# Value weights folded into the output weights, in an encoder layer of attention and mLSTM

## The chip, the cores and the metric

The kernel runs on one core of one Trainium2 chip (trn2). The metric is device time in microseconds (us), the median of a few executions. PE is the engine for matmuls, DVE (VectorE), ACT (ScalarE) and POOL (GpSimd) work on tiles of 128 partitions, and SP (SyncE) issues most DMAs. SPq and ACTq are the queues of DMAs that SP and ACT issue.

## What is computed

```python
def mla_group(c_q, c_kv, k_pe, cos, sin, g_cq, g_ckv, w_uq, w_ukv, g_q, g_k):
    q = (rms_norm(c_q, g_cq) @ w_uq).reshape(B, S, A_HEADS, A_DH)
    kv = (rms_norm(c_kv, g_ckv) @ w_ukv).reshape(B, S, A_HEADS, A_NOPE + A_DV)
    k_nope, v = kv[..., :A_NOPE], kv[..., A_NOPE:]
    ...
    # softmax(q k^T * scale) v per head, all queries see all keys

def reference(x, ...):
    h = rms_norm(x, g_mix_norm[l])
    z = h @ w_in[l]
    q_m, k_m, v_m, o_m, gates, c_q, c_kv, k_pe = jnp.split(z, splits, axis=-1)
    ...
    y_a = mlstm_group(q_m, k_m, v_m, o_m, gates, b_gates[l], g_mlstm_out[l])
    y_b = mla_group(c_q, c_kv, k_pe, cos, sin, ...)
    x = x + jnp.concatenate([y_a, y_b], axis=-1) @ w_out[l]
    h = rms_norm(x, g_ffn_norm[l])
    x = x + jnp.square(jax.nn.relu(h @ w_ff1[l])) @ w_ff2[l]
```

There are 2048 tokens, a model width of 1024, four attention heads with 128 value columns, 128 key columns and 64 rotary columns each, and a latent `c_kv` of 128 columns, from which keys and values of all heads are made. All in float32.

## The kernel before

Every float32 product is made of three matmuls: each operand is split into a high part (`kh`, a cast on ACT) and the rest (`kl`, a subtraction on DVE or POOL), by `split`, and `mm3` adds high x high, low x high and high x low. "A product" below is three such matmuls, if nothing else is said.

The first phase makes the input projection z for the two halves of the tokens. A half has three blocks (`CV`, `CQ`, `CO`: value, query-and-key, out-gate columns) of eight token tiles each. A slot is one such tile, 24 matmuls. Into the slots `tick` sets the stages of the attention's latent work for a token tile t: `mla_a1` normalises the latents (`cn`), transposes and splits them (`cTh`, `cTl`); `mla_a2` multiplies them by the split weights `wukh`, `wukl` (128 x 1024: for each head 128 key and 128 value columns) in two products of 512 columns, `pk`; `mla_b1` copies the value columns out of `pk` (`vn`, on ACT) and stores them to `d_va` in DRAM; `mla_b2` transposes queries and keys and stores them (`d_qn`, `d_qr`, `d_kn`, `d_kr`). In this phase a scheduler sets the order of instructions on each engine. The out-gate slots end in a sigmoid and a store `d_sg<-vo`.

Attention follows, in the order in which it is written. It runs 16 blocks (four heads by four query blocks of 512 queries), 16 scores each; g counts the 256 scores. A score is five matmuls of 128x512 (three for the 128 key columns, two for the rotary ones, `rh`, `rl`, `qr`) into one of three banks `ps`. DVE copies it out and takes its maximum (`p`), ACT takes exponentials, PE transposes the probabilities, ACT and DVE split them (`pth`, `ptl`), and PE multiplies them with a split value block (`vh`, `vl`) in `pv`, 22 scores later. `load_q`, `load_k` and `load_v` bring raw queries, keys and values of a head into tiles `raw` of a pool of eight stage tiles; `split_q`, `split_k` and `split_v` split them. At the start `load_q(0, 0)`, the four `load_k(0, j)` and their splits stand ahead of everything else; later heads are loaded and split at fixed scores. The mLSTM group runs between the scores, as a generator `work`; its first part is `mlstm_prelude`. After attention, `OutProj` multiplies by `w_out` (rows 0 to 511 for mLSTM, the rest for attention), and the feed-forward layers follow.

A tile may lie on memory of another one that is no longer read; then the first instruction that writes it waits for the last one that read the old tile. Each DMA also takes one of eight completion lanes in turn (`DMAHW0` to `DMAHW7` in the order's rows) and waits until the DMA that had the lane before has landed.

## Time and profile before

| | |
|---|---|
| median of 3 runs | 2543.5 us (2543.17 to 2545.29) |
| profiled execution | 2542.08 us |
| its span in the trace | 2540.3 us |
| granted clock of PE | 1.00 |
| PE busy | 2523.7 us (99%) |
| DVE busy | 1726.1 us (68%) |
| ACT busy | 1293.7 us (51%) |
| POOL busy | 380.7 us (15%) |

Times inside the kernel are counted from the start of the span. The first phase ends and attention begins at about 458 us; attention ends at about 1122 us. Busy shares are averages over these stages.

### The profile page before, as it was taken

The page shows a single profiled execution, that of the slowest core. Times are in us where ns is not written, and L with a number is a line of the kernel's source. Part 1 is how long each engine was busy: PE and PEld are TensorE (multiplying, and loading weights), DVE is VectorE, ACT ScalarE, POOL GpSimd, SP SyncE. Part 2 cuts the span into 40 slices and gives each one's busy share as a digit, 9 for nine tenths or more (in the row PEclk, how much of TensorE's full clock was granted, in tenths as well). Part 3 has the DMA queues.
Part 4 walks back from the last instruction along what each step waited for, and adds up shares of the span by engine and source line. Part 5 has one row for each costly group of instructions (what it writes and reads, how often), then busy time and mean ns, then how long its engine had stood idle before and what let it go on. Part 6 is the DMA issues. An engine that isn't in the chain of part 4 may idle for free. (4 is left out here: it accounts for less than half of the span.)

```text
span 2540.3 us, 35812 instructions
## 1 busy us (share of the span) xinstructions
PE 2523.7 (99%) x12380; PEld 2111.3 (83%) x12380; DVE 1726.1 (68%) x3286; ACT 1293.7 (51%) x2900; POOL 380.7 (15%) x428
## 2 busy tenths in 40 slices
PE   9999999999999999999999999999999999999999
PEld 7888888788888888888888888888888888888887
DVE  5585467766667667678788777977775577665433
ACT  6454444656767677674455555655554323332332
POOL 1211111223323332200000000000000232322000
PEclk9999999999999999999999999999999999999999
DMA  5434234355344343235786555654448544444552
GB/s 177 143 112 152 91 113 137 111 146 134 89 115 114 85 121 102 63 110 193 235 271 227 196 189 185 244 166 149 142 153 300 201 149 142 145 145 145 211 183 95
DMA packets 295931, 392.53 MB, mean 155 GB/s; under 512 B 32262, under 2 KB 176965, under 8 KB 295749
## 3 DMA queue, kind: packets, MB, share of 16 engines
q1 hardware_dynamic: 293284, 385.78, 48.0%
q10 hardware_dynamic: 2464, 4.46, 0.5%
q8 instruction: 97, 1.59, 0.3%
q14 instruction: 86, 0.70, 0.1%
HBM read 258.51 MB, written 131.64 MB: 154 GB/s over the span
## 5 line engine op out<-in xcount | busy, mean ns | idle before, releaser
L69 PE MATMUL pd<-w2h,uh 128*128 128x512 f32 x896 | 348.8, 389 | 0.1
L70 PE MATMUL pd<-w2l,uh 128*128 128x512 f32 x896 | 348.7, 389 | 0.0
L71 PE MATMUL pd<-w2h,ul 128*128 128x512 f32 x896 | 348.7, 389 | 0.0
L54 DVE TENSOR_TENSOR ul<-ur,uh 128x1024 fp32r<-128x1024 f32 x110 | 149.3, 1357 | 251.8 <-ACT uh L53 251.8
L53 ACT CAST uh<-ur 128x1024 fp32r<-128x1024 f32 x110 | 115.7, 1052 | 396.0 <-PE pd L70 382.4
L54 DVE TENSOR_TENSOR ptl<-ptp,pth 128x512 fp32r<-128x512 f32 x248 | 171.1, 691 | 190.0 <-ACT pth L53 188.9
L53 ACT CAST pth<-ptp 128x512 fp32r<-128x512 f32 x248 | 143.4, 578 | 157.7 <-PE ptp L1137 157.1
L2015 DVE TENSOR_TENSOR e<-pu,e 128x512 f32<-128x512 f32 x224 | 151.3, 689 | 88.7 <-PE pu L71 87.7
L69 PEld LDWEIGHTS pd<-w2h,uh 128*128 128x128 f32 x896 | 168.2, 188 | 35.4 <-DVE e L2015 0.5
L71 PEld LDWEIGHTS pd<-w2h,ul 128*128 128x128 f32 x896 | 168.2, 188 | 34.9
L70 PEld LDWEIGHTS pd<-w2l,uh 128*128 128x128 f32 x896 | 168.2, 188 | 34.8
L1106 ACT ACTIVATE p<-p,nm 128x512 f32<-128x512 f32 x256 | 185.8, 726 | 2.6 <-DVE nm L1099 2.6
L1095 DVE TENSOR_SCALAR_CACHE_REDUCE p<-ps 128x512 f32<-128x512 f32 x256 | 167.4, 682 | 15.2 <-PE ps L1094 15.1
L2179 POOL TENSOR_TENSOR r<-wr,r 128x512 f32<-128x512 f32 x48 | 81.5, 1697 | 621.1 <-DMA wr<-in_w 590.0
L69 PE MATMUL pz<-wh,hh 128*128 128x512 f32 (+1 forms) x384 | 149.5, 391 | 1.7 <-ACT vo L495 0.7
L71 PE MATMUL pz<-wh,hl 128*128 128x512 f32 (+1 forms) x384 | 150.0, 391 | 0.0
L70 PE MATMUL pz<-wl,hh 128*128 128x512 f32 (+1 forms) x384 | 149.2, 389 | 0.1
L2018 ACT ACTIVATE e<-e 128x512 f32<-128x512 f32 x128 | 80.9, 632 | 120.5 <-DVE e L2015 114.0
L1137 PE MATMUL ptp<-ident,p 128*128 128x128 f32 x992 | 130.6, 274 | 0.5 <-DVE ptl L54 0.3
L1137 PEld LDWEIGHTS ptp<-ident,p 128*128 128x128 f32 x992 | 113.6, 140 | 14.1 <-issue 1.4
L1090 PE MATMUL ps<-kh,qh 128*128 128x512 f32 x256 | 112.8, 441 | 2.4 <-DVE p L1095 2.4
L1883 ACT CAST r<-w1raw 128x512 fp32r<-128x512 f32 x104 | 64.6, 622 | 92.5 <-PE pu L71 92.5
(526 smaller groups left out, 6463.5 us busy)
## 6 DMA issues: line engine op xcount, KB each, us to landing
d_u<-e SPq DMA_DIRECT2D x224, 256.0 KB
ur<-d_u SPq DMA_DIRECT2D x110, 512.0 KB
wr<-in_w SPq DMA_DIRECT2D x96, 256.0 KB
w1raw<-in_w SPq DMA_DIRECT2D x42, 512.0 KB
raw<-in_w_in SPq DMA_DIRECT2D x48, 256.0 KB
r<-in_w SPq DMA_DIRECT2D x22, 512.0 KB
mb<-d_M SPq DMA_DIRECT2D x32, 256.0 KB
acc<-d_x SPq DMA_DIRECT2D x16, 512.0 KB
```

The lines of the kernel that those rows point to most:

```text
L53: r = nc.scalar.copy(hi, src)
L54: (eng or nc.vector).tensor_tensor(lo, src, hi.bitcast(F32), op=ALU.subtract)
L69: nc.tensor.matmul(out, ah, bh, start=first, stop=False, skip_group_check=more)
L70: nc.tensor.matmul(out, ah, bl, start=False, stop=False, skip_group_check=more)
L71: nc.tensor.matmul(out, al, bh, start=False, stop=last, skip_group_check=more)
L1090: nc.tensor.matmul(o, qh[:, qs], kh, start=True, stop=False)
L1095: nc.vector.tensor_scalar(p, o, SCALE, None, op0=ALU.mult, op1=ALU.max, accum_out=maxes[b, a][:, j:j + 1])
L1106: nc.scalar.activation(p, p, AF.Exp, bias=maxes[b, a], accum_out=dens[b][:, a, j:j + 1])
L1137: nc.tensor.transpose(pt[:, k, :], p[:, k * P:(k + 1) * P], c.ident)
L2015: nc.vector.tensor_tensor(out, o, t, op=ALU.add)
L2018: nc.scalar.activation(t, t, AF.Relu)
L2179: nc.gpsimd.tensor_tensor(R, wr, R, op=ALU.subtract)
```

## The change

Attention's result of a head is the weighted sum of value rows, and these are latents times the head's value weights. The head's rows of `w_out` come behind. The changed kernel multiplies the two weights once, W'(h) = W_value(h) x W_out(h) (128 x 1024), and lets attention sum latents.

- `load_wu` splits only the key columns of `w_ukv` into the first 512 columns of `wukh` and `wukl`; `mla_a2` makes one product of 512 columns for keys. `mla_b1` no longer copies and stores values. `mla_a2` stores the 128 latent columns of `cn` to `d_cn`, on ACT's queue.
- `value_rows` runs in the slots n = 13 to 23 of the second half, one step a slot: it loads `w_ukv` again, scales and transposes its value columns (four transposes), splits them into the other 512 columns of `wukh` and `wukl`, loads `w_out`'s rows of the heads in eight pieces, splits each into a token tile `xt`, and makes eight products of 128x512, one a slot. Each result is copied on ACT and stored to `d_wv` on ACT's queue.
- Attention loads four value blocks once for all heads, from `d_cn`, in place of four for each head. Their loads stand at g = 2 to 8 and their splits (cast on ACT, subtraction on POOL) at g = 16 to 22; before, they were loaded ahead of the scores and split at g = 6 to 12, and again for each head at the end of the one before.
- The split of the next head's key block 2 (u = 5) goes from POOL to DVE.
- The mLSTM's first loads of values and keys come at the eleventh step of the prelude, no longer ahead of it, and later ones at the step before.
- `OutProj` reads `d_wv` where it read rows 512 and on of `w_out`.

```diff
             for j in range(2):
-                raw = rp.tile([P, 512], F32, name="raw")
-                cs = slice(j * 512, (j + 1) * 512)
-                nc.sync.dma_start(raw, c.w_ukv[:, cs])
-                split(nc, wukh[:, cs], wukl[:, cs], raw, gcq[:, 2:3])
+                raw = load_ukv(j)
+                cs = slice(j * 256, (j + 1) * 256)
+                split(nc, *[w[:, cs].rearrange("p (h d) -> p h d", h=2) for w in (wukh, wukl)],
+                      raw[:, :, 0, :], gcq[:, 2:3])
+
...
+        def value_rows():
+            raws = [load_ukv(j) for j in range(2)]
+            yield
+            for raw in raws:
+                nc.scalar.activation(raw[:, :, 1, :], raw[:, :, 1, :], AF.Copy, scale=gcq[:, 2:3])
+            pt = psT.tile([P, 4, P], F32, name="pt")
+            for h in range(NH):
+                nc.tensor.transpose(pt[:, h, :], raws[h // 2][:, h % 2, 1, :], c.ident)
+            split(nc, wukh[:, 512:], wukl[:, 512:], pt.rearrange("p h d -> p (h d)"))
+            yield
+            pieces = {}
+
+            def load(n):
+                h, j = divmod(n, 2)
+                pieces[n] = rp.tile([P, 512], F32, name="raw")
+                nc.sync.dma_start(pieces[n], c.w_out[512 + h * P:512 + (h + 1) * P, j * 512:(j + 1) * 512])
+
+            def part(n):
+                t = xp.tile([P, D], F32R, name="xt")
+                wh, wl = t[:, 0:512], t[:, 512:D]
+                split(nc, wh, wl, pieces.pop(n))
+                if 0 < n and n + 3 < 2 * NH:
+                    load(n + 3)
+                parts.append((wh, wl))
+
+            parts = []
+            load(0)
+            part(0)
+            yield
+            for n in range(1, 4):
+                load(n)
+            for n in range(2 * NH):
+                h, j = divmod(n, 2)
+                if n + 1 < 2 * NH:
+                    part(n + 1)
+                wh, wl = parts.pop(0)
+                o = psM.tile([P, 512], F32, name="pm")
+                hs = slice(512 + h * P, 512 + (h + 1) * P)
+                mm3(nc, o, wukh[:, hs], wukl[:, hs], wh, wl, True, True)
+                w = ep.tile([P, 520], F32, name=("ot", "zc")[j])[:, 0:512]
+                nc.scalar.copy(w, o)
+                nc.scalar.dma_start(c.d_wv[h * P:(h + 1) * P, j * 512:(j + 1) * 512], w)
+                yield
...
-            zr, ms3, ch, cl = mla_env[t]
-            pk, pq = [], []
-            for j in range(2):
-                o = psM.tile([P, 512], F32, name="pm")
-                cs = slice(j * 512, (j + 1) * 512)
-                mm3(nc, o, ch[:, 2, :], cl[:, 2, :], wukh[:, cs], wukl[:, cs], True, True)
-                pk.append(o)
+            zr, ms3, ch, cl, cn = mla_env[t]
+            nc.scalar.dma_start(c.d_cn[t * P:(t + 1) * P, :], cn[:, 256:384])
+            pq = []
+            pk = psM.tile([P, 512], F32, name="pm")
+            mm3(nc, pk, ch[:, 2, :], cl[:, 2, :], wukh[:, 0:512], wukl[:, 0:512], True, True)
...
-            vn = mp.tile([P, NH, DV], F32, name="vn")
-            for j in range(2):
-                nc.scalar.copy(vn[:, 2 * j:2 * j + 2, :],
-                               pk[j].rearrange("p (h d) -> p h d", h=2)[:, :, NOPE:])
-            nc.sync.dma_start(c.d_va[tok, :], vn.rearrange("p h d -> p (h d)"))
...
                     tick(n + 6 * half)
+                    if half and n >= 13:
+                        next(rows, None)
...
-        load_v(0, 0)
-        load_v(0, 1)
         work = mlstm()
...
                 if h < NH - 1 and i == 7 and u in (4, 5, 6):
-                    split_k(h + 1, u - 3, nc.vector if u == 6 else nc.gpsimd)
-                    if u == 6:
-                        load_v(h + 1, 0)
-                        load_v(h + 1, 1)
+                    split_k(h + 1, u - 3, nc.gpsimd if u == 4 else nc.vector)
...
-                if g in (6, 8, 10, 12):
-                    split_v(0, g // 2 - 3)
-                    if g < 10:
-                        load_v(0, g // 2 - 1)
+                if g in (2, 4, 6, 8):
+                    load_v(g // 2 - 1)
+                if g in (16, 18, 20, 22):
+                    split_v(g // 2 - 8)
...
-            nc.sync.dma_start(raw, c.w_out[k * P:(k + 1) * P, :])
+            nc.sync.dma_start(raw, c.d_wv[(k - 4) * P:(k - 3) * P, :])
```

The order in which SP issues DMAs shows where the loads of attention's first tiles stand (`raw<-d_qn` and `raw<-d_qr` are its queries, `raw<-d_kn` and `raw<-d_kr` its keys; the names in brackets are what an instruction waits for, a lane first). In the kernel before they begin among the last stores of the latent attention's queries (L407):

```order
L1064 DMA raw_4984<-d_qn_78 128x512 [waits DMAHW2_49,PE_49]
L1067 DMA raw_4986<-d_qr_80 64x512 [waits DMAHW3_49]
L1067 DMA raw_4986<-d_qr_80 64x512 [waits DMAHW4_49]
L1033 DMA raw_4989<-d_kn_79 128x512 [waits DMAHW5_49]
L1036 DMA raw_4991<-d_kr_81 64x512 [waits DMAHW6_49]
L407 DMA d_qn_78<-qT_4378 128x4x128 [waits DMAHW7_49,Activation_49]
L1036 DMA raw_4991<-d_kr_81 64x512 [waits DMAHW0_49]
L1033 DMA raw_5001<-d_kn_79 128x512 [waits DMAHW1_49]
```

In the changed kernel they stand in one piece behind the last store of the mLSTM's keys (L521), and go on in this way to the fourth key block:

```order
L521 DMA d_k_75<-kt_4538 2x128 [waits DMAHW1_49,Activation_49]
L1110 DMA raw_4982<-d_qn_78 128x512 [waits DMAHW7_49]
L1113 DMA raw_4984<-d_qr_80 64x512 [waits DMAHW0_49,PE_49]
L1113 DMA raw_4984<-d_qr_80 64x512 [waits DMAHW2_49]
L1080 DMA raw_4987<-d_kn_79 128x512 [waits DMAHW3_49]
L1083 DMA raw_4989<-d_kr_81 64x512 [waits DMAHW4_49]
L1083 DMA raw_4989<-d_kr_81 64x512 [waits DMAHW6_49]
L1080 DMA raw_4999<-d_kn_79 128x512 [waits DMAHW7_49]
L1083 DMA raw_5001<-d_kr_81 64x512 [waits DMAHW0_49]
L1083 DMA raw_5001<-d_kr_81 64x512 [waits DMAHW1_49]
```

The loads have moved behind the stores, and the wait for PE from the first load to the second.

On PE, the kernel before has four matmuls of the first score (`ps`) ahead of the last out-gate tile's product (`pz_4856`, 24 matmuls):

```order
L70 MATMUL pz_4827<-wl_4679,hh_2702 128x512
L71 MATMUL pz_4827<-wh_4678,hl_2703 128x512
L1090 MATMUL ps_5054<-kh_5006,qh_4994 128x512
L1091 MATMUL ps_5054<-kl_5007,qh_4994 128x512
L1092 MATMUL ps_5054<-kh_5006,ql_4995 128x512
L1093 MATMUL ps_5054<-rh_5010,qr_4998 128x512
L69 MATMUL pz_4856<-wh_4636,hh_2702 128x512
```

In the changed kernel the last folded product (`pm_4876`, on a piece of `w_out` in `xt`) stands in the last out-gate tile's product (`pz_4883`), and the first score comes behind both:

```order
L70 MATMUL pm_4876<-xt_4837,wukh_157 128x512
L71 MATMUL pm_4876<-xt_4837,wukl_158 128x512
L70 MATMUL pz_4883<-wl_4574,hh_2647 128x512
L71 MATMUL pz_4883<-wh_4573,hl_2648 128x512
L69 MATMUL pz_4883<-wh_4579,hh_2647 128x512
L70 MATMUL pz_4883<-wl_4580,hh_2647 128x512
L71 MATMUL pz_4883<-wh_4579,hl_2648 128x512
L69 MATMUL pz_4883<-wh_4585,hh_2647 128x512
L70 MATMUL pz_4883<-wl_4586,hh_2647 128x512
L71 MATMUL pz_4883<-wh_4585,hl_2648 128x512
L1136 MATMUL ps_5048<-kh_5004,qh_4992 128x512
L1137 MATMUL ps_5048<-kl_5005,qh_4992 128x512
```

Behind the last matmul that reads `wukl` stand eight of the first phase, and no score stands among them any more.

## Rows read from the trace of the kernel before

**Rows 1.** The page's part 1, busy time, share and instructions.

```profile
PE 2523.7 (99%) x12380; PEld 2111.3 (83%) x12380; DVE 1726.1 (68%) x3286; ACT 1293.7 (51%) x2900; POOL 380.7 (15%) x428
```

**Rows 2.** Windows by stage: busy time of PE, PEld, DVE, ACT, POOL, clock.

```profile
0.00:458.00 458.00, 450.30 (x2235) 382.74 (x2236) 286.33 (x736) 224.59 (x651) 73.39 (x128) 1.00 0.42 134
458.00:490.00 32.00, 29.89 (x147) 23.49 (x146) 27.77 (x83) 25.04 (x58) 7.80 (x6) 1.00 0.48 132
490.00:1122.00 632.00, 631.16 (x3665) 536.04 (x3664) 426.49 (x1091) 428.92 (x1202) 171.09 (x182) 1.00 0.40 106
```

**Rows 3.** PE's waits: total, times, longest.

```profile
PE ps L1090 <- DVE p L1095: 2.4, 4, 1.3
```

**Rows 4.** Timeline of PE, 455 to 484: start, duration, [idle before].

```profile
457.74 0.39 PE L71 MATMUL pz<-wh,hl 128*128 128x512 f32 x1
457.96 0.39 PE L1094 MATMUL ps<-rl,qr 128*128 128x512 f32 x1
...
461.31 0.39 PE L1090 MATMUL ps<-kh,qh 128*128 128x512 f32 x1
...
466.55 0.39 PE L1093 MATMUL ps<-rh,qr 128*128 128x512 f32 x1
...
471.25 0.50 PE L1090 MATMUL ps<-kh,qh 128*128 128x512 f32 x1 [0.69 <-DVE p L1095]
...
480.30 0.50 PE L1090 MATMUL ps<-kh,qh 128*128 128x512 f32 x1 [1.34 <-DVE p L1095]
...
481.56 1.04 PE L1137 MATMUL ptp<-ident,p 128*128 128x128 f32 x8
```

**Rows 5.** PE's groups by form, 0 to 458: busy, mean ns.

```profile
L69 PE MATMUL pm<-wukh,cTh 128*128 128x512 f32 x32 | 13.0, 408 | 0.0
```

**Rows 6.** ACT's value copies: duration ns min, median, max.

```profile
L369 ACT COPY vn<-pm x32: 351/365/401, 62.7 to 420.6; 128x256 f32<-128x256 f32 x32
```

**Rows 7.** Timeline of ACT, 425 to 476.

```profile
447.44 0.62 ACT L53 CAST kh<-raw 128x512 fp32r<-128x512 f32 x1 [0.94 <-DMA raw<-d_kn]
```

**Rows 8.** Timeline of DVE, 440 to 490.

```profile
450.38 0.68 DVE L54 TENSOR_TENSOR rl<-raw,rh 128x512 fp32r<-128x512 f32 x1
...
468.23 0.28 DVE L647 TENSOR_TENSOR d<-d,wi 128x128 f32<-128x128 f32 x1
468.62 1.20 DVE L649 TENSOR_TENSOR ln<-ln,d 128x128 f32<-128x128 f32 x1
...
476.20 3.45 DVE L671 TENSOR_TENSOR_SCAN mr<-g 1x15 f32<-1x15 f32 x8
```

**Rows 9.** Timeline of POOL, 440 to 476.

```profile
468.37 1.30 POOL L54 TENSOR_TENSOR vl<-raw,vh 128x512 fp32r<-128x512 f32 x1 [13.25 <-PE ps L1094]
```

**Rows 10.** Timeline of PE, 764 to 782, a head's end.

```profile
777.93 0.66 PE L1137 MATMUL ptp<-ident,p 128*128 128x128 f32 x4 [0.33 <-DVE ptl L54]
```

**Rows 11.** Timeline of SP, 425 to 480: start and time of issue.

```profile
428.31 0.46 SPq L1064 DMA_DIRECT2D raw<-d_qn  x1
...
439.53 1.13 SPq L1036 DMA_DIRECT2D raw<-d_kr  x2
...
442.51 0.53 SPq L1033 DMA_DIRECT2D raw<-d_kn  x1
443.14 1.08 SPq L1036 DMA_DIRECT2D raw<-d_kr  x2
...
460.46 0.24 SPq L479 DMA_DIRECT2D d_k<-kt  x1
461.96 0.32 SPq L735 DMA_DIRECT2D knat<-d_k  x1
```

**Rows 12.** SP's waits, 395 to 480: total, times, longest.

```profile
SPq L735 <- DMA d_k<-kt: 1.1, 1, 1.1
```

**Rows 13.** DMA, 425 to 450: packets, bytes, rate.

```profile
DMA packets 6057, 6.01 MB, mean 240 GB/s; under 512 B 535, under 2 KB 4006, under 8 KB 6054
```

**Rows 14.** Timeline of PE, 0 to 12.

```profile
4.69 1.97 PE L163 MATMUL pt<-ident,xt 128*128 128x128 f32 x8
```

## What was predicted

> **What bounds the kernel now.** I read the page first, then the windows by stage, then PE's waits, then the timelines of all engines where the first phase ends and attention begins. The page gives the profiled execution 2540.3 us of span, with PE busy for 2523.7 of it [rows 1]. The windows by stage repeat this for each stage: 450.30 of 458 us in the first phase, 631.16 of 632 in most of attention, always at granted clock 1.00, and the one stretch that is visibly less full is 458 to 490, with 29.89 of 32 [rows 2]. So PE's stream of instructions sets the time, and only two things can change it: matmuls taken out or put in, and moments at which PE stands. PE's largest wait after the start, 2.4 us in four pieces, is for VectorE's score evacuation `p` [rows 3], and nearly all of it lies in that one stretch, 0.69 us at 471.25 and 1.34 us at 480.30 [rows 4].
>
> The shown duration of a matmul (0.39) overlaps its neighbours. What it costs is the distance of starts: from 461.31 to 466.55 there are 23 steps in 5.24 us, 0.228 us each [rows 4].
>
> **PE's work: -5.0 us.** The key-and-value product of a token tile was two 128x512 products of three matmuls. The listing shows 32 of one kind [rows 5] and as many of the two others, 96 in all, and the key half needs 48. The 48 value ones go. Eight products of three come in to make the folded weights: 24 matmuls of the same shape. Net 24 x 0.228 = 5.5 us less. Four transposes come in; eight take 1.04 us [rows 4], so four are put at 0.5. Together -5.0. Attention's own value product keeps its shape (128 latent columns in place of 128 value columns), and so do scores, output projection and FFN: nothing.
>
> **Work of the others in the first phase: 0, bounds 0 to +2.** 32 copies `vn` of 0.365 us leave ScalarE (11.7 us) [rows 6]. In come 8 casts and 8 copies of 128x512, priced by a cast of 0.62 us [rows 7], and 24 more DMA issues there. VectorE gets some ten splits of about 0.68 us [rows 8]. The cover is PE, busy all through: ScalarE works 224.59 and VectorE 286.33 of these 458 us [rows 2]. One product's chain (cast, split, three matmuls, copy) is some 0.62 + 0.68 + 0.7 + 0.62 = 2.6 us, against about 5.5 us of PE work in a slot (24 matmuls x 0.228). If the cover fails once or twice, by the chain's length less nothing, that is up to 2 us. I take 0, since the slot's own z matmuls lie between.
>
> **Value loads and splits in attention: -1.0, bounds -2 to 0.** Sixteen per-head loads and splits become four, and the four move from scores 6 to 12 to scores 16 to 22. They all lie off PE's path in the middle of attention (631.16 of 632), so their number saves nothing there. But at 468.62 VectorE's `ln` takes 1.20 us where its like at 468.23 takes 0.28 [rows 8], just while GpSimd's value subtraction runs from 468.37 for 1.30 us [rows 9]; the wait of 0.69 us at 471.25 follows. Without it VectorE gains 0.9 us. The wait at 480.30 comes from eight scans of 3.45 us at 476.20 [rows 8], which stay. So 0.69 to 0.9 and a little of the second wait: 1.0. If the time falls on other instructions, 0; if both waits go, 2. The Trainium skill ("GPSIMD Engine Reference", section Specifications) says that GpSimd and VectorE share their way to SBUF and that VectorE's instructions with two SBUF inputs are slowed; `ln` has two, and the trace agrees with its 1.20 us.
>
> **The key split moved from GpSimd to VectorE: 0, bounds 0 to +1.** At three head boundaries VectorE gets two subtractions of 0.68 us, 1.4 us, in slots where PE waits a little already (0.33 us at 777.93) [rows 10]. PE has three score banks, which hide about as much. A third of a us each if not.
>
> **The start of attention: +7.4, bounds +5.7 to +9.1, and 0 if a reason is wrong.** This is the term that decides. Before, SyncE issues the first query and key loads from 428.31 to 444.22 (443.14 and 1.08) [rows 11], 30 to 14 us ahead of 457.96, where the last z matmul's successor starts [rows 4]. The order shows four score matmuls even ahead of the last z products. In the changed order the second of these loads (the query's rotary part) has a wait for PE. Its stage tile lies on bytes of `wukl`, and counted out, the wait is for the last matmul of the last folded product `pm_4876`, eight matmuls ahead of the end of the first phase. Before, the last readers of these weights were MLA's products of the last token tile, slots earlier. Call the end of the first phase T. The load can be issued at T - 1.65 (eight matmuls x 0.228, less the drain), and behind it in SyncE's queue stand all others: 14 DMAs up to the last key block.
>
> Issue alone: from 439.53 to 444.22 eight such DMAs take 4.69 us, 0.58 each with their gaps [rows 11]. Fourteen take 8.2, so the last is issued by T + 6.5. Landing takes between 1.5 us (a lone store, issued 460.46; the load that reads it could start at 461.96, after a wait of 1.1 for it) [rows 11, 12] and 4.9 us (a key block issued at 442.51, for which ScalarE's cast at 447.44 waited 0.94) [rows 7, 11]. Then come the cast (0.62), the subtraction (0.68), and, since VectorE's order puts the first `p` behind the split of the last key block, one `p` of 0.68 before the fourth score has a bank: 2.0. So the fourth score starts between T + 10.0 and T + 13.4. Unhindered it starts at T + 4.3: before, at 461.31, 3.35 us after 457.96 [rows 4], and four score matmuls (0.9) were done ahead. Delay 5.7 to 9.1 us. The loads are 2.36 MB; in 425 to 450 the queues moved 240 GB/s [rows 13], at which they take 9.8 us, between the two ends. I take the middle, 7.4. The Trainium skill ("DMA: Bandwidth & Descriptors", section Bandwidth) puts what one core draws from HBM near 358 GB/s, and by it the loads would take 6.6 us, less than their issue, and the delay would be the low end, 5.7, with a total of 2543.2; the trace's 240 speaks for more.
>
> What is late next: `p` and softmax of the first four scores, and through them everything of attention by the same amount. VectorE and ScalarE stand in that time, so nothing is made up later.
>
> **Sum.** The profiled execution took 2542.08. 2542.08 - 5.0 - 1.0 + 7.4 = 2543.5. The median of the runs is 1.4 above that execution, so the forecast is 2544.9 us, +1.4 or 0.05%: no change. A measurement of this kernel can tell about 0.2%, 5.1 us.
>
> **Rivals.**
> 1. *The loads are hidden anyway.* If the counted wait is satisfied earlier, or the scores find the data in time, then -5.0 - 1.0 stands alone: 2537.5, faster. For it: the change is fewer matmuls on a PE-bound kernel, and all else before T has cover. Against it: PE's wait on the second load stands in the order, and 14 to 30 us of lead are gone. Chance 0.17.
> 2. *The loads come one behind the other through the completion lanes (slower).* The order shows each DMA waiting for one of eight lanes in turn, that is for the landing of the one eight before it. If landing takes L, the 14th lands at T - 1.65 + 13 L/8 + L, and the delay is 2.625 L - 3.95: 8.9 us at the 4.9 of [rows 7, 11]. Stores of the last results (`d_sg`, `d_wv`) use the same lanes. From L = 5.7 us on the sum is 5.1 above the median, and the kernel is slower; at L = 6.3 the delay is 12.6 and the time 2550.1. For it: 4.9 us was seen with half of this traffic in loads. Against: while PE stands nothing else moves. Chance 0.23.
> 3. *The clock falls while PE stands.* PE waits from T to its first new score: five DMAs to T + 1.3, landing 1.5 to 4.9, cast and split 1.3, so 4 to 7.5 us at a stretch. At the program's start, after 4.5 us without work, eight transposes take 1.97 us [rows 14] against 1.04 later [rows 4], half speed, at 1.2 in place of 2.4 GHz. If that happens for the first 4 us of scores, it costs up to half of this, 1.9: 2546.8, still no change. Against: after the 1.34 us wait at 480.30 the clock was 1.00, but that stretch was short. Chance 0.25. The Trainium skill ("TensorE: Matmul & The Clock Gate", section HAM oscillation) says that a kernel whose PE stands for a transfer falls back to half clock and must win it again; by it this case would be 2546.8.
> 4. The forecast as it stands: 0.35.
>
> **Numbers.** Within 0.2%: 0.35 + 0.25 = 0.60. Faster: 0.17. Slower: 0.23. The range leaves out a tenth on either side: 2537.5, where rival 1 has its middle, to 2550.5, which holds most of rival 2. The forecast's own range, by its delay of 5.7 to 9.1 and the terms of 0 to +2 and 0 to +1, is 2543 to 2549.
>
> **What would show it.** Right: the listing shows 48 and 24 matmuls in place of 96; PE's rows stand between the last z matmul and the first score for 4 to 7 us, with the wait put down to VectorE's or ScalarE's split; SyncE's first rotary query load is issued within 2 us of T, and the loads follow at 0.58; the window from T to 30 us on has 7 us less PE busy; `ln` takes 0.3. Wrong: scores that follow the last z matmul at once; a granted clock under 1.00 in that stretch (rival 3); loads further apart than 0.6 (rival 2); PE waits inside the slots of the folded products, or at the head boundaries.

## The result, and the profile after

The changed kernel takes 2556.3 us (median of 6 runs, 2555.18 to 2559.61), the kernel before 2543.6 beside it. The ratio is 1.0050, interval 1.0039 to 1.0061: slower by 12.8 us, outside the range of 2537.5 to 2550.5. The profiled execution took 2558.85 us with a span of 2556.9. It lies 2.5 us above its own median and that of before 1.5 below, so the terms below, read from the two profiles, add up to 16.6 and not 12.8.

The page and the windows by stage answer to [rows 1, 2]:

```profile
PE 2527.2 (99%) x12360; PEld 2111.0 (83%) x12360; DVE 1727.9 (68%) x3301; ACT 1294.8 (51%) x2875; POOL 352.1 (14%) x410
```

```profile
0.00:458.00 458.00, 445.67 (x2200) 378.24 (x2201) 285.38 (x737) 224.81 (x628) 68.72 (x120) 1.00 0.41 131
458.00:490.00 32.00, 23.43 (x88) 16.55 (x86) 18.07 (x51) 19.20 (x38) 4.91 (x9) 0.84 0.84 214
490.00:1122.00 632.00, 630.41 (x3652) 534.72 (x3651) 431.49 (x1118) 424.19 (x1194) 155.83 (x169) 1.00 0.39 95
...
200.00:250.00 50.00, 48.29 (x245) 41.28 (x243) 26.09 (x59) 26.69 (x62) 7.53 (x15) 0.97 0.48 148
```

In the kernel before, the same stretch from 200 to 250 us was full:

```profile
200.00:250.00 50.00, 50.00 (x262) 43.02 (x261) 27.45 (x65) 26.75 (x65) 7.30 (x15) 1.00 0.49 157
```

PE is less busy in two places: 445.67 in place of 450.30 in the first phase, 23.43 in place of 29.89 at the start of attention, where the granted clock is 0.84. From 490 to 1122 it differs by 0.75 us only. PE's waits (total, times, longest) give the releasers, and PE's timeline their places:

```profile
PE ps L1136 <- ACT kh L53: 6.1, 1, 6.1
PE pz L69 <- ACT vo L537: 2.8, 1, 2.8
PE ps L1136 <- DVE p L1141: 2.3, 2, 1.9
```

```profile
240.34 1.03 PE L164 MATMUL pt<-ident,xt 128*128 128x128 f32 x8
243.14 0.47 PE L69 MATMUL pz<-wh,hh 128*128 128x464 f32 x1 [0.92 <-ACT hh L53]
244.61 0.89 PE L164 MATMUL pt<-ident,xt 128*128 128x128 f32 x4 [0.78 <-DVE hl L54]
...
413.12 0.50 PE L69 MATMUL pz<-wh,hh 128*128 128x512 f32 x1 [2.83 <-ACT vo L537]
...
460.23 0.39 PE L71 MATMUL pz<-wh,hl 128*128 128x512 f32 x1
466.73 0.79 PE L1136 MATMUL ps<-kh,qh 128*128 128x512 f32 x1 [6.12 <-ACT kh L53]
...
476.40 0.47 PE L1136 MATMUL ps<-kh,qh 128*128 128x512 f32 x1 [1.93 <-DVE p L1141]
```

Two places in PE's timeline, the last z matmul and the fourth score, cut the difference of 16.6 us into three. Before, the last z matmul started at 457.74 and the fourth score at 461.31 [rows 4]; four score matmuls (0.9 us) were done ahead of the former. With these 0.9 and the 5.0 of saved PE work taken off, the last z should start at 451.8.

- **First phase:** it starts at 460.23, 8.4 us late.
- **Start of attention:** from there to the fourth score are 16.2 us; before, 3.6 and the 0.9, 4.5. So 11.7 late.
- **The rest:** from the fourth score to the end 2080.5 in place of 2079.0, 1.5.

8.4 + 11.7 + 1.5 - 5.0 = 16.6.

What held the loads shows on SP, in its timeline and in its waits from 440 to 476:

```profile
397.36 6.25 SPq L179 DMA_DIRECT2D raw<-in_w_in  x4
404.52 0.45 SPq L292 DMA_DIRECT2D raw<-in_w_out  x1
...
458.82 1.15 SPq L1113 DMA_DIRECT2D raw<-d_qr  x2
460.01 0.58 SPq L1080 DMA_DIRECT2D raw<-d_kn  x1
...
468.38 1.08 SPq L1083 DMA_DIRECT2D raw<-d_kr  x2
```

```profile
SPq L1113 <- PE pm L71: 10.3, 1, 10.3
...
SPq L1083 <- DMA raw<-d_kn: 1.4, 1, 1.4
...
SPq L1080 <- DMA d_sg<-vo: 0.8, 1, 0.8
...
SPq L1080 <- DVE rl L54: 0.4, 1, 0.4
```

The wait counted out of the order is there, and the load behind it starts at 458.82. That is 1.64 us ahead of 460.46, the end of the first phase (the start of the last z matmul and 0.23; the forecast's T, with 1.65 forecast). Behind it the loads wait for lanes (of an earlier load and of a `d_sg` store) and for a stage tile (`rl`). ACT's timeline shows when the last load had landed, and the DMA line of 458 to 476 the rate:

```profile
408.34 0.62 ACT L53 CAST xt<-raw 128x512 fp32r<-128x512 f32 x1 [1.80 <-DMA raw<-in_w_out]
412.46 0.61 ACT L537 ACTIVATE vo<-pz 128x512 f32<-128x512 f32 x1
...
474.31 0.62 ACT L53 CAST rh<-raw 128x512 fp32r<-128x512 f32 x1 [0.61 <-DMA raw<-d_kr]
```

```profile
DMA packets 2640, 3.94 MB, mean 219 GB/s; under 512 B 327, under 2 KB 848, under 8 KB 2640
```

So the 16.2 us are: issue up to 469.46, 9.2 behind the start of the last z and 9.0 behind T (forecast 6.5); landing 4.85 to the cast at 474.31 (forecast 1.5 to 4.9); 2.1 of cast, subtraction and `p` (forecast 2.0). The forecast's 4.9 was counted from the start of an issue; counted so, this landing takes some 5.4.

### The profile page after: what moved, and what is told of

It reads as the page before. It is cut to its first block, busy times and chain, and to the rows that moved or that the text cites. A ratio compares the mean times of both kernels' runs of the same rounds, so it can differ in the third digit from the quotient of the medians.

```text
span 2556.9 us, 35737 instructions
## 1 busy us (share of the span) xinstructions
PE 2527.2 (99%) x12360; PEld 2111.0 (83%) x12360; DVE 1727.9 (68%) x3301; ACT 1294.8 (51%) x2875; POOL 352.1 (14%) x410
## 5 line engine op out<-in xcount | busy, mean ns | idle before, releaser
L1141 DVE TENSOR_SCALAR_CACHE_REDUCE p<-ps 128x512 f32<-128x512 f32 x256 | 167.3, 681 | 12.9 <-PE ps L1140 12.8
L1183 PEld LDWEIGHTS ptp<-ident,p 128*128 128x128 f32 x992 | 113.4, 140 | 15.8 <-DVE ptl L54 2.9
```

The lines of the kernel that those rows point to most:

```text
L1141: nc.vector.tensor_scalar(p, o, SCALE, None, op0=ALU.mult, op1=ALU.max, accum_out=maxes[b, a][:, j:j + 1])
L1183: nc.tensor.transpose(pt[:, k, :], p[:, k * P:(k + 1) * P], c.ident)
```

## The experiments

The theory at first: the 11.7 us come from the stage tiles on `wukl`'s memory; the first phase's wait at 413 from the late first piece of `w_out`. Rivals: the completion lanes, the folded products themselves, the clock. Each diff is against the changed kernel, if nothing else is said, and lines left out are marked by dots. Each result gives the median, its ratio to the kernel before, and the interval. The kernel before, measured again beside the experiments, lay between 2544.2 and 2546.0 (2543.6 beside the changed kernel), so medians of two experiments can differ by 1 to 2 us for nothing; the ratios don't have this.

**The weights' tiles moved** (`wukh` and `wukl` are made at the start of their pool, so no stage tile lies on them).

```diff
+        wukh = kp.tile([P, 1024], F32R, name="wukh")
+        wukl = kp.tile([P, 1024], F32R, name="wukl")
...
-        wukh = kp.tile([P, 1024], F32R, name="wukh")
-        wukl = kp.tile([P, 1024], F32R, name="wukl")
```

> The changed kernel with the split key-and-value weights placed elsewhere in SBUF, so that no stage tile of attention's first loads lies on them. Theory 1 (the second load waits for the last folded product's reader of wukl, and the whole load queue behind it): the loads are issued more than 8 us ahead of the end of the first phase, the wait of 6.1 us before the first score and the 1.9 us before the fourth go, and the time falls by about 10 us to 2546. Rival (the loads come late by the lanes and by the traffic of the last stores, whatever memory they write): the loads end within 4 us of where they ended, and the time stays at 2554 to 2557.

2554.83, ratio 1.0038 [1.0025, 1.0050]. The time forecast for the theory was missed. The first score waits 3.0 us in place of 6.1, but the fourth starts 12.6 behind the last z. SP's waits show what came next: the lanes of two stores.

```profile
SPq L1083 <- DMA d_wv<-ot: 4.6, 1, 4.6
SPq L1113 <- DMA d_sg<-vo: 2.6, 1, 2.6
```

Taking away the memory alone gains little, since the lanes hold the loads next.

**Folded rows stored through GpSimd's queue, alone and with the tiles moved.**

```diff
-                nc.scalar.dma_start(c.d_wv[h * P:(h + 1) * P, j * 512:(j + 1) * 512], w)
+                nc.gpsimd.dma_start(c.d_wv[h * P:(h + 1) * P, j * 512:(j + 1) * 512], w)
```

> The changed kernel with the stores of the folded weights (d_wv) on GpSimd's queue, so that the first loads of attention no longer take their completion lanes after them. The wait on wukl stays. Two covers lie over each other here. Theory 2 (the load queue is held by the wait on wukl and, behind it, by the lanes of the last d_wv stores; either alone holds it): as the wait on wukl is still there, the second load is issued 1.6 us ahead of the first phase's end as before and the time falls by at most 2 us, 2554 to 2557. Rival (the lanes alone do it): the time falls by 5 us or more.

2554.96, 1.0042 [1.0029, 1.0054]. No clear gain alone.

> The changed kernel with both covers taken away: weights placed off the stage tiles as in the run on memory, and d_wv stored from GpSimd's queue. Theory 2: all loads up to the fourth key block's first are issued 8 us or more ahead of the first phase's end; the fourth block's rotary load still waits for the lane of the last out-gate store. The wait before the first score falls from 6.1 to some 3 us, which ScalarE's and VectorE's splits behind the last sigmoid need, the fourth score comes 8 us after the end in place of 16, and the time falls by 6 to 9 us, to 2547 to 2550. Rival (the traffic of the products itself makes the loads late): less than 3 us.

2555.24, 1.0037 [1.0024, 1.0050]: missed. The first loads are issued at 449.45 and 451.27, ahead of the last z, but later ones stand 7.4 and 3.6 us on the lanes of `d_sg` stores, and the fourth score starts 12.1 behind.

**The `d_sg` stores on GpSimd's queue too,** on top of both.

```diff
-            nc.scalar.dma_start(c.d_sg[t * P:(t + 1) * P, :], o)
+            nc.gpsimd.dma_start(c.d_sg[t * P:(t + 1) * P, :], o)
```

> Both covers taken away as before, and the out-gate stores (d_sg) on GpSimd's queue too, so that no load of attention waits for a store by its lane. Theory 2: the fourth key block is no longer late, the fourth score comes 6 to 7 us after the first phase's end, and the time falls by another 1 to 2 us, to 2546 to 2548. What is left at the start is the chain of ten casts on ScalarE (0.52 us each) behind the last sigmoid. Rival: the stores from GpSimd's queue are slow or disturb VectorE, and the time is not under that of the run with both covers.

2549.59, 1.0023 [1.0015, 1.0032], short of the forecast. Of these four versions, only the one with memory and both sets of stores out of the way lets the loads run ahead. The fourth score starts 9.9 us behind the last z, still not 4.5. So the start gained 3.6, 0.7, 4.1 and 6.3 of its 11.7 us in the four profiled executions, while the last z came 2.1 later, 1.9 earlier, 2.6 later and 1.5 earlier than in the changed kernel; the medians hold both. PE's timeline, and DVE's:

```profile
458.72 0.39 PE L71 MATMUL pz<-wh,hl 128*128 128x512 f32 x1
460.82 0.50 PE L1136 MATMUL ps<-kh,qh 128*128 128x512 f32 x1 [1.71 <-ACT kh L53]
...
468.57 0.47 PE L1136 MATMUL ps<-kh,qh 128*128 128x512 f32 x1 [1.23 <-DVE p L1141]
```

```profile
463.04 1.78 DVE L54 TENSOR_TENSOR rl<-raw,rh 128x512 fp32r<-128x512 f32 x1
464.74 1.76 DVE L54 TENSOR_TENSOR kl<-raw,kh 128x512 fp32r<-128x512 f32 x1
```

These two subtractions run beside GpSimd's for the third key block (462.93 to 465.96) and take 1.78 and 1.76 us in place of 0.68.

**The last key block in two tiles of another pool,** on top of the one before (`d_sg`), since its load waited for a stage tile.

```diff
+            kst, kname = (pp, "p") if (h, j) == (0, 3) else (rp, "raw")
-            raw = rp.tile([P, 512], F32, name="raw")
+            raw = kst.tile([P, 512], F32, name=kname)
...
```

> Both covers away, the out-gate stores on GpSimd's queue, and the raw fourth key block in two tiles of the probabilities' pool; the pieces of the output weights stay on ScalarE and VectorE. Theory 2: of the 9.8 us from the last z matmul to the fourth score in the run without this, some 2 us were the fourth block's loads, which waited for the queries' splits to free their stage tiles; they go, the fourth score comes 7 to 8 us after the last z matmul, and the time is 2547 to 2548.5. What stays is the chain of casts behind the last sigmoid. Rival (the splits set the pace, not these loads): 9 us or more, 2549 to 2551.

2551.16, 1.0024 [1.0015, 1.0033]; fourth score 9.1 behind, as the rival had it. Nothing gained but 0.7 us at the start: now the casts and subtractions set the pace. They stand behind the last sigmoid in ACT's and DVE's order; in the kernel before they stood between those of the first phase from 437 on.

**GpSimd splits pieces of `w_out`:** first all eight, on the version with the `d_sg` stores moved.

```diff
-                split(nc, wh, wl, pieces.pop(n))
+                raw = pieces.pop(n)
+                nc.gpsimd.tensor_copy(wh, raw)
+                nc.gpsimd.tensor_tensor(wl, raw, wh.bitcast(F32), op=ALU.subtract)
```

> The run with both covers away and the out-gate stores on GpSimd's queue, and with the pieces of the output weights split on GpSimd (cast and subtraction) in place of ScalarE and VectorE. Theory 4 (the wait of 3 us at 413 in the changed kernel is ScalarE standing, in its order, at the cast of the first piece, with the out-gate's sigmoid behind it): that wait goes, and the time falls by 2 to 4 us from 2549.6 to 2546 to 2548. Rival (GpSimd, at 1.3 us an operation, becomes late itself, holds the latent's reciprocal roots behind it and the stage tiles of the next weights): no gain or slower, with new waits of PE for weights.

2553.49, 1.0030 [1.0018, 1.0042]. The wait at 413 falls from 2.9 to 1.5, but GpSimd's pieces come late and the last product starts at 461.09, 7.5 us behind the last z, as the rival had it. With the last key block's tiles too:

> As the run with the pieces split on GpSimd, and with the raw fourth key block in two tiles of the probabilities' pool, so that its loads no longer wait for the queries' split. Theory 2: all loads are issued ahead of the first phase's end; what is left at the start is the chain of ten casts behind the last sigmoid, the fourth score comes at about 7 us after the end in place of 9.8, and the time is 1 to 3 us below that run. Rival: the fourth score waits for VectorE's splits as long as before, no gain.

2552.71, 1.0030 [1.0019, 1.0041]. No gain. Then only the first two pieces (`n < 2`) on GpSimd, with those tiles:

> As the run with the fourth key block in other tiles, and with the first two pieces of the output weights, whose casts stand ahead of the latent work on ScalarE, split on GpSimd; the other six stay. Theory 4: the wait of about 3 us near 410 goes or falls under 1 us, nothing is late at the end of the first phase, and the time falls by 2 to 4 us to 2543 to 2546, about that of the kernel before. Rival (ScalarE's squares of the last latent tiles are late in any case): the wait stays over 1.5 us and the time within 1 us of that run.

2546.15, 1.0007 [0.9998, 1.0016]: 5 us better than with the key block's tiles alone (2551.16), and no difference from the kernel before is shown. The fourth score (465.31) is 9.1 behind the last z (456.18) as without it, so the gain lies in the first phase, where the last z comes 5.2 earlier. The wait by 410 fell from 3.8 to 1.6; PE's waits from 395 to 420, without and with the edit:

```profile
PE pz L69 <- ACT vo L537: 3.8, 1, 3.8
...
PE pz L69 <- ACT vo L542: 1.6, 1, 1.6
```

That is 2.2 of the 5.2. The clock is the greater part of the rest: without the edit the granted clock is 0.66 from 410 to 420, and the first twelve z matmuls behind the wait start 0.43 us apart in place of 0.23, which costs 2.5 us; with it the clock stays at 1.00. The changed kernel itself has 1.00 there behind its wait of 2.8 us, so it has only the wait to lose.

**The first piece of `w_out` loaded a slot earlier.**

```diff
-            raws = [load_ukv(j) for j in range(2)]
...
             pieces = {}
...
+            raws = [load_ukv(j) for j in range(2)]
+            yield
...
             load(0)
+            pt = psT.tile([P, 4, P], F32, name="pt")
...
+            yield
             part(0)
```

> The changed kernel with the first piece of the output weights loaded one slot earlier than it is split. Theory 1 (ScalarE stands in its order at the cast of the first piece, whose load was issued in the same slot, and so gives the out-gate's sigmoid late): the wait of 2.8 us before 413 falls under 1 us and the time by about 2 us to 2554. Rival (ScalarE has too much work in this slot, load or not): the wait stays over 2 us, the time at 2556.

2557.09, 1.0044 [1.0032, 1.0057]. The wait stayed, at 3.1. SP still comes to this load behind the four of `w_in` whose issue takes 6.24 us (396.68, then 403.83), and the cast waits 2.14 us for it. A step earlier in the code was no earlier on the queue.

**Two slots earlier for everything.**

```diff
-                    if half and n >= 13:
+                    if half and n >= 11:
```

> The changed kernel with the folded products two slots (11 us) earlier, in slots 11 to 21. Theory 1: the wait on wukl ends 11 us earlier, most of the first loads land ahead of the first phase's end, and the time falls by 7 to 10 us to 2546 to 2549; products meet the last latent token tiles, which may cost up to 2 us of it. Rival (lanes and traffic): less than 3 us.

2563.51, 1.0071 [1.0059, 1.0084]: 7 us worse by the medians (5 by the ratios), where a gain was expected. The steps now fall among the last latent tiles:

```profile
PE pt L441 <- DVE kn L425: 5.1, 1, 5.1
PE pz L69 <- ACT wh L56: 2.7, 3, 1.0
```

But the start of attention is whole again, with the folding kept: the loads are issued from 447.77 to 461.46, the casts of queries and keys stand ahead of the last sigmoids, and the scores follow the last z at once.

```profile
480.54 0.39 PE L71 MATMUL pz<-wh,hl 128*128 128x512 f32 x1
480.76 0.39 PE L1136 MATMUL ps<-kh,qh 128*128 128x512 f32 x1
...
485.00 0.39 PE L1136 MATMUL ps<-kh,qh 128*128 128x512 f32 x1
```

The fourth score is 4.5 us behind the last z, so all of the 11.7 us are gained, and the last z starts 20.3 us later (460.23 to 480.54). Theory 1 was right on the start; its price for the latent tiles, up to 2 us, was wrong.

**No folding.** `value_rows` isn't run and the output projection reads plain `w_out` for attention's rows, so the value half of the weights is left out of the computation.

```diff
-                        next(rows, None)
+                        pass
...
-            nc.sync.dma_start(raw, c.d_wv[(k - 4) * P:(k - 3) * P, :])
+            nc.sync.dma_start(raw, c.w_out[k * P:(k + 1) * P, :])
...
```

> The changed kernel without the weight folding: its transposes, splits, products and stores are left out, and the output projection reads the plain output weights, so attention's latents are multiplied by weights that lack the value half. PE has 24 matmuls and four transposes less, 6.0 us. Theory 1 (all of the loss hangs on the folding: 10 us at the start of attention, 2 us at 413): 2556.3 - 6.0 - 12 = 2538 or less, down to 2532 if the rest of the first phase's loss is the folding's too. Rival (part of the loss comes from the latent stores and the changed order of the first phase): 2540 to 2545, with waits in the first phase that stay.

2536.07, 0.9961 [0.9947, 0.9975], as theory 1 had it. The scores follow the last z at once and the fourth is 4.5 us behind it, as much as before:

```profile
451.91 0.39 PE L71 MATMUL pz<-wh,hl 128*128 128x512 f32 x1
452.14 0.39 PE L1136 MATMUL ps<-kh,qh 128*128 128x512 f32 x1
...
456.39 0.39 PE L1136 MATMUL ps<-kh,qh 128*128 128x512 f32 x1
```

So the folding costs 2556.3 - 2536.1 = 20 us by the medians (22.6 by the ratios, 21.1 between the two profiled spans), of which its PE work is 6.0 (24 x 0.228 + 0.5). The rest are waits that it makes: of the 21.1, the 11.7 at the start, 2.4 in the first phase and 1.1 behind the fourth score.

The rival is right in part too. Without value products and without folded ones PE has 48 matmuls less, 10.9 us, so the last z should start at 457.74 - 0.9 - 10.9 = 445.9. It starts at 451.91. So 6.0 of the 8.4 us that the first phase is late are there without the folding.

**PE kept busy ahead of the scores** by 56 transposes that nobody reads.

```diff
+        pm = psM.tile([P, 512], F32, name="pm")
+        for n in range(56):
+            nc.tensor.transpose(pm[:, n % 4 * P:(n % 4 + 1) * P], c.ident, c.ident)
```

> The changed kernel with 56 transposes of the identity (0.11 us each at full clock, 6.2 us) on PE ahead of the first score, whose results nobody reads, so that PE works while it waits for the first keys. Theory 3 (part of the loss at the start is the clock: it falls while PE stands, and scores run at half speed behind the wait): the granted clock in the 30 us behind the first phase rises from 0.84 to near 1.00, the first scores follow each other at 0.23 us in place of 0.43 and more, and the time falls by 1 to 3 us, to 2553 to 2555. Rival (the slow scores wait for keys anyway, the clock costs nothing): the clock rises and the time stays within 1 us of 2556.

2560.83, 1.0058 [1.0046, 1.0071]. The clock stays at 1.00 up to 470, and the fourth score still comes 16.3 us behind the last z (461.16), as with the clock down:

```profile
455.00:470.00 15.00, 14.14 (x90) 12.00 (x88) 4.06 (x6) 4.88 (x9) 0.00 (x0) 1.00 0.60 175
470.00:490.00 20.00, 17.36 (x67) 12.23 (x67) 13.94 (x41) 14.83 (x30) 3.93 (x9) 0.91 0.91 225
```

```profile
468.32 0.48 PE L1136 MATMUL ps<-kh,qh 128*128 128x512 f32 x1
...
477.45 0.47 PE L1136 MATMUL ps<-kh,qh 128*128 128x512 f32 x1 [1.75 <-DVE p L1141]
```

The half-speed scores cost nothing while the next keys are waited for. The time met neither forecast: its median is 4.5 above the changed kernel's, but the two intervals of the ratio overlap and the two profiled spans differ by 0.2 us (2557.1 and 2556.9), so no loss is shown, and no gain.

**The value and key-split part alone, on the kernel before:** loads at g = 2 to 8, splits at 16 to 22, u = 5 on DVE.

```diff
-        load_v(0, 0)
-        load_v(0, 1)
...
-                if g in (6, 8, 10, 12):
-                    split_v(0, g // 2 - 3)
-                    if g < 10:
-                        load_v(0, g // 2 - 1)
+                if g in (2, 4, 6, 8):
+                    load_v(0, g // 2 - 1)
+                if g in (16, 18, 20, 22):
+                    split_v(0, g // 2 - 8)
```

> The kernel before with two of the small moves alone: the first head's value loads at scores 2 to 8 and their splits at 16 to 22, and the next head's key block 2 split on VectorE. By the prediction's terms (-1.0 with bounds -2 to 0, and 0 to +1): 2542.5 to 2545, VectorE's ln at 0.3 us in place of 1.2 and the first of the two waits for p gone. Rival (the value splits meet other work on VectorE, or key splits cost at the head boundaries): 1 us or more slower.

2544.32, 0.9994 [0.9985, 1.0003]: 1.0 us below the median of the kernel before beside it (2545.31), 1.5 by the ratio. That agrees with the term of -1.0 but doesn't show it, since the interval holds 1. PE's waits for `p` are down from 2.4 to 0.4, but two new ones for GpSimd's `kw` take 2.0. DVE's timeline answers to [rows 8]: `ln` 0.29 in place of 1.20, the eight scans 1.88 in place of 3.45.

```profile
468.98 0.29 DVE L649 TENSOR_TENSOR ln<-ln,d 128x128 f32<-128x128 f32 x1
...
475.64 1.88 DVE L671 TENSOR_TENSOR_SCAN mr<-g 1x15 f32<-1x15 f32 x8
```

**The start of the second half.** From 200 to 250 us PE is 1.7 us less busy, at clock 0.97. The changed kernel's order puts eight transposes together at 240.34 with four z matmuls behind them, and the next z matmul waits for their split; before, four and four stood with products between. The run without folding has the same eight (240.03) and waits 1.4 and 0.4, so the folding isn't the cause. Behind the two waits, 1.7 us, eight matmuls start 0.39 apart in place of 0.21, some 1.4 us more. First the `d_cn` stores were moved to SP's queue:

```diff
-            nc.scalar.dma_start(c.d_cn[t * P:(t + 1) * P, :], cn[:, 256:384])
+            nc.sync.dma_start(c.d_cn[t * P:(t + 1) * P, :], cn[:, 256:384])
```

> The changed kernel with the latent stores (d_cn) on SyncE's queue in place of ScalarE's. Theory 2b (the wait of some 3.5 us at 243, which the kernel without products has too, comes from ScalarE standing for the latent stores' input): that wait falls under 1 us, the time by 2 to 4 us to 2552 to 2554. Rival (it comes from the changed order of ScalarE's and VectorE's work there, store or not): it stays, 2556.

2555.83, 1.0040 [1.0026, 1.0054]; the waits stay (0.35 and 1.24). Then the latents were copied into a tile of their own, so that `cn` is free earlier; this was to bring the spread order back.

```diff
+            vc = mp.tile([P, P], F32, name="vc", bufs=2)
+            nc.scalar.copy(vc, cn[:, 256:384])
...
-            nc.scalar.dma_start(c.d_cn[t * P:(t + 1) * P, :], cn[:, 256:384])
...
+            nc.scalar.dma_start(c.d_cn[t * P:(t + 1) * P, :], vc)
```

> The changed kernel with one thing added: the 128 latent columns of a token tile are copied on ScalarE into a tile of their own, and the store to d_cn reads this copy, one stage later. In the order the second eight transposes of the second half's first tiles are four and four again, with products between, as in the kernel before. The new tile also moves other tiles' memory, so that the second query load waits no more for the last reader of the split weights, as in the run with the weights' tiles moved (2554.83). If the order of the transposes is the cause of the 3 us that the changed kernel loses from 200 to 250 us, PE has 49.9 busy there or more in place of 48.29, no wait at 243 and 244, and the time is 3 us under that run: 2551 to 2552. Rival: the loss lies in something else that the scheduler has moved, or comes back in a later slot, and the time stays at 2554 to 2556.

2557.56, 1.0043 [1.0029, 1.0056]. Eight transposes still stand together (239.08), but eleven z matmuls are behind them in place of four, and the next waits 0.50. The windows show the loss of that place mostly gone, and PE's timeline that it came back at the end:

```profile
200.00:250.00 50.00, 49.46 (x258) 42.44 (x257) 27.24 (x63) 27.31 (x64) 8.09 (x15) 1.00 0.49 159
...
458.00:490.00 32.00, 21.51 (x78) 15.00 (x78) 17.67 (x51) 19.00 (x36) 4.88 (x9) 0.79 0.89 227
```

```profile
456.47 0.51 PE L69 MATMUL pm<-xt,wukh 128*128 128x512 f32 x1 [0.88 <-ACT xt L53]
...
466.94 0.79 PE L1138 MATMUL ps<-kh,qh 128*128 128x512 f32 x1 [8.02 <-ACT kh L53]
...
476.47 0.47 PE L1138 MATMUL ps<-kh,qh 128*128 128x512 f32 x1 [1.82 <-DVE p L1143]
```

The folded products have become the first phase's last work (458.53), the first score waits 8.0 us, and the fourth starts at 476.47 as in the changed kernel. The text expected the wait of the load for the weights' reader to be gone; it is there (3.3 us, load issued at 458.96). The same on the best version:

> The last version so far (weights' tiles moved, stores of d_wv and d_sg on GpSimd's queue, the last key block in tiles p, two pieces split on GpSimd; 2546.15) with the same copy added. If the order of the transposes is worth 3 us there too, 2543, level with the kernel before. Rival: 2545.5 to 2546.5, if the 3 us are something else.

2553.33, 1.0030 [1.0018, 1.0041]: 7 us worse than the same without the copy, though 200 to 250 is full (50.00 in place of 48.31) and the transposes stand four and four. The loads start at 451.26, behind stores of mLSTM's keys for which SP waits 8.7 us for ACT, and the fourth score is 15.7 behind the last product (454.93). Last, the third key block's subtractions on VectorE, so that its others don't run beside GpSimd's:

```diff
-            split_k(0, j, nc.gpsimd if j == 2 else nc.vector)
+            split_k(0, j, nc.vector)
```

> The same, and the third key block's subtractions on VectorE in place of GpSimd, so that VectorE's two subtractions beside it take 0.68 us each in place of 1.78 and 1.75, and two more of 0.68 come in. If that sharing delays the fourth score, it starts some 0.8 us earlier behind the last z product (9.1 to 8.3) and the time is 0.8 us under the run without it: about 2542. Rival: VectorE's line of splits is as long as before, and nothing changes, within 0.5 us.

2554.0, 1.0032 [1.0019, 1.0044], no gain; the fourth score is 15.8 behind the last product. So the third block's place on GpSimd is not what sets the start there. Whether it does where the loads are early (subtractions of 1.78 and 1.76) wasn't tried.

## Why the prediction was wrong

**PE's work, -5.0: right.** The listing from 0 to 462 has 16 and 8 in place of 32 of its kind:

```profile
L69 PE MATMUL pm<-wukh,cTh 128*128 128x512 f32 x16 | 6.7, 416 | 0.0
L69 PE MATMUL pm<-xt,wukh 128*128 128x512 f32 x8 | 3.4, 426 | 0.0
```

**Work of the others in the first phase, 0 to +2: this step failed.** It came to 8.4 in the profiled execution. The step took the cover from averages: ACT half idle, PE full. Its bound was also below its own chain, which makes 2.6 us for one failure and 5.2 for two, not 2. What the runs show in its place:

- ACT takes its instructions in their order. At 408.34 its cast of the first piece waits 1.80 us for a load that SP could issue only behind 6.25 us of `w_in` loads, and the squares of the latents and the sigmoid at 412.46, for which PE stands 2.83 us (0.69 before), are behind it. With two pieces off ACT and DVE this wait fell by 2.2, and the last z came 5.2 earlier.
- The stretch from 200 to 250 us lost some 3 us (1.7 of standing, and the low clock behind it) by an order that the folding didn't make. Copying the latents filled it, and cost more elsewhere.
- At the program's start 2.0 us are lost: ACT's first copy of z, `zr`, comes at 17.5 in place of 15.6. In the other versions of the changed kernel it is 0.4 to 2.1 late, so how much of it is this execution's stays open.
- The rest, some 1 us, isn't placed.

The run without folding gives the same term in two parts: 6.0 that come with the change's other edits and this execution, and 2.4 that come with the folding.

**Start of attention, +7.4, bounds 5.7 to 9.1: the mechanism is right, the size too small, 11.7.** The forecast's chain holds link by link, but the issue ended 9.0 behind T and not 6.5, since the loads also wait for lanes and stage tiles, and the landing was 4.85, the upper end and not the middle of 3.2. 2.5 + 1.65 + 0.1 is 4.25 of the 4.3 that are missing. Rival 2 had the lanes, and its price for L = 4.9 (8.9) was still too low. What the prediction lacked altogether is that the causes lie one behind the other. Taking away the memory gave 1.5 us by the medians, the stores of `d_wv` alone 1.4, both no more, both and `d_sg` 6.7, and then the splits set the pace. Where the loads came early enough, with everything two slots earlier, all of the 11.7 was gone.

**Rival 3, the clock,** came true in the rows (0.84 from 458 to 490, the matmuls behind the wait of 6.1 us 0.43 apart) but not in the price: at the start of attention it cost at most the 1.5 us behind the fourth score. The Trainium skill ("TensorE: Matmul & The Clock Gate", section HAM oscillation) has the fall to half clock for a PE that stands for a transfer. The trace agrees, with the 0.84 behind 6.1 us without work. What the fall costs depends on whether PE is what is waited for. At the first scores it isn't, as the filler run shows. In the first phase it is: some 1.4 us behind the waits at 243 and 244, and 2.5 in the run with the key block's tiles. The prediction looked for the clock only at the start of attention.

**The rate.** The queues moved 219 GB/s in 458 to 476, near the 240 of [rows 13]. The Trainium skill ("DMA: Bandwidth & Descriptors", section Bandwidth) has 358 for one core. The highest stretch read here is the first 12 us of the changed kernel, 312, and the low end that was built on the 358 wasn't reached.

**Value loads and splits, -1.0:** 1.0 to 1.5 by its own run, in an interval that holds nothing too. `ln` takes 0.29 as forecast. The scans, which the prediction held fixed at 3.45 us, take 1.88 in that run and 0.77 in the changed kernel, so their length was GpSimd's doing too. **Key split, 0:** in that run too, and no wait of its own is seen there.

**The verdict** had a chance of 0.23 through rival 2 alone. The two failed terms were put down as independent and small. All of the start's 11.7 and 2.4 of the first phase's 8.4 come with the folding, whose steps meet ACT's order and SP's queue at that place; the other 6.0 don't.

Open: a place for the folded products that meets neither the last latent tiles (slots 11 to 21) nor attention's first loads (13 to 23). No version with the folding beat the kernel before.

## What to carry to other kernels

Work that is put into the slots of a saturated engine is priced by what stands behind it on the in-order engines and queues at that place, not by their average idle time. If a prefetch has to wait for late work, list all that it waits for (memory, lanes, stage tiles, the splits behind it), since taking away one only shows the next. Where a scheduler sets the order, look at the whole order again after every small edit: one 128-column copy filled the stretch from 200 to 250 us (48.3 to 50.0 busy) and made the whole 7 us longer.

## What the runs showed of the hardware

A load's issue waited 4.6 us for an unrelated store's landing, through the lane they share in turn.

VectorE's eight scans on one partition, 15 elements each, take 0.77 us in the changed kernel, where GpSimd does nothing meanwhile. They take 1.88 with one GpSimd subtraction on 64 partitions beside them (the kernel before with the value part alone) and 3.45 with GpSimd subtracting all the while (the kernel before). Subtractions of 0.68 us take 1.78; [rows 8] had shown this for `ln` only.

```profile
492.07 0.77 DVE L716 TENSOR_TENSOR_SCAN mr<-g 1x15 f32<-1x15 f32 x8
```

A fall of the clock behind a wait costs time only where nothing else is waited for: 2.5 us behind 3.8 us without work in the first phase, at most 1.5 behind 6.1 us at the first scores.
